# The first pass of each MLP takes two column blocks by seven products, sums of products kept apart, SBUF laid out with pads

## The chip, the cores and the metric

The kernel runs on one core of one Trainium2 chip. The engines that matter are TensorE (PE in the profile; PEld is its loading of weights), VectorE (DVE), ScalarE (ACT), GpSimd (POOL, almost unused) and SyncE (SP), whose queue issues nearly all transfers. The metric is device time in microseconds (us), less is better. The kernel before takes 2031.8 us, the median of three runs (2031.58 to 2032.2).

## The reference

Two layers over 256 tokens of width 2048, all in fp32. Each sub-layer ends in a layer norm over the scaled residual:

```python
for layer in range(DEPTH):                       # 2
    mix = short_conv_mixer(h, ...) if layer < N_A else mla_mixer(h, ...)
    h = layer_norm(ALPHA * h + mix, ln_g[layer, 0], ln_b[layer, 0])
    h = layer_norm(ALPHA * h + sq_relu_mlp(h, mlp_w1[layer], mlp_w2[layer]), ln_g[layer, 1], ln_b[layer, 1])

def sq_relu_mlp(x, w1, w2):                      # 2048 -> 8192 -> 2048
    return jnp.square(jax.nn.relu(x @ w1)) @ w2
```

The first layer mixes by a gated convolution, the second by latent attention with 16 heads. The change sits in the two MLPs (called idx 1 and idx 3 in the code, after the number of the norm that follows).

## The kernel before, in words

**Precision.** A matrix product is made from fp32r halves. `split` (L114) turns a tile into a high half (ScalarE, L116, a cast) and a low half (VectorE, L117, source minus high half); a product of two split operands is three matmuls: high with high, high with low, low with high (`dot`, L274 to L278). Where one operand has both halves side by side, the first two are one wide matmul (`mm_run`, L198).

**Weights.** All weights come once, as tiles of 128 x 1024 (512 KB), in the order of one list, `stream`. `take` (L166) hands out the next tiles and prepares those that follow, at most LOOK = 5 tiles ahead: `prepare` (L130) issues the load on SP's queue and splits the tile. There are five raw buffers and eight pairs of split ones.

**An MLP.** The 8192 hidden values are done in NQ = 8 passes (q) of QC = 8 chunks of 128. A pass first makes its eight chunks: each is 16 x 2 matmuls over the 2048 inputs (`products`, L265; L192 high, L196 low), taken out of PSUM, through relu and square, and split into `h` (`hidden`, L593). It then multiplies them into the output: `down` (L288) takes one block of 512 columns out of four, for both halves t of the tokens and all eight chunks: 16 products of three matmuls of 512 columns, 48 in all. `put` (L575) adds the result to `acc`, in the first pass by a copy on ScalarE (L577).

**The first pass (q = 0)** differs: the layer norm ahead of the MLP is not ready when its matmuls start, so the hidden products run on the un-normalised values with the norm's gain and offset as two additional columns (`mm_wide`, L219), and `ln.weighted` (L477 to L484) applies the norm's factors to the sums. These factors come from `ln.finish` (L448); the first hidden chunk is evacuated once they are there. Beside it the input itself is normalised for the later passes: `normal` (L567, which calls `ln.normal`, L465) for 16 chunks, each three VectorE steps (L470, L471, L475) and two on ScalarE (L472, L474). The code calls it once per hidden chunk after the first, and twice at each `put` of the pass.

**Seven products.** In the passes of FAST, before the change q = 1 to 6, blocks 0 and 1 are done together by a Strassen-like scheme: chunks are paired, a pair of chunks by two token halves is a 2 x 2 matrix, the weights of two chunks by two blocks another, and seven products replace eight. For one pair of chunks the weights' forms are made in `prepare` from two raw tiles: three splits of 1024 columns, a 1024-wide difference (L149), two 512-wide differences (L152, L155) and a split of 512. The hidden forms are four 128-wide sums (L605 to L608) and one split per pair. `down_fast` (L316) does 4 pairs x 7 products x 3 = 84 matmuls of 512 columns instead of 96, and `combine` (L642) adds the seven sums into the four places of `acc`.

**Ends of the MLPs.** The last pass is plain. In the first MLP `to_wide` (L658) turns the blocks back and starts the next norm (`prepare_all`, L680, subtracts a first mean from all 16 chunks of the residual; `begin` calls it at the head of the last pass). In the second MLP `to_out` (L911) normalises the output; its gain and offset, `gbt`, are loaded by GpSimd's queue (L914), and the residual is turned and added by `turn_residual` (L903) once per pass, ahead of the last block.

**Order.** The code is handed to a framework that schedules instructions for each engine from its own estimate of times and inserts semaphores; the order of each engine in the built program is then fixed, and an engine takes its instructions one after the other. PSUM has eight banks, handed out in turn (`psum`, L180).

## Time and profile before

| | |
|---|---|
| median of three runs | 2031.8 us |
| profiled execution | 2031.86 us, of which the span is 2030.0 us |
| TensorE busy | 2022.8 us |
| VectorE busy | 1637.1 us |
| ScalarE busy | 1186.2 us |
| first MLP's passes | 386 to about 1020 us |
| second MLP's passes | 1345 to 2030 us (the output's norm included) |
| granted TensorE clock | 1.00 in all stretches shown |

The profile is of one execution. Its busy times are per engine; its rows give the code's line (L117), the engine, the operation, and the program's names of the tiles written and read (`lo<-raw,hi`); "ps_u" are the sums of hidden products, "ps_d" those of `down`, "ps_f" those of the seven products, "raw" a weight tile as loaded, "hi" and "lo" its halves. A row of a view over time begins with the start in us and the duration; the bracket at the end says how long the engine was idle before and what ended it. A row of a view of one tile or line has count, shortest, median and longest duration in ns, and the first and last start. Matmuls overlap, so the step from one start to the next is shorter than the duration.

### The profile page before, as it was taken

The numbers are of one execution on the slowest core, as the hardware profiler recorded it, in microseconds if no ns is written. First come the engines' busy times: TensorE is split into PE (matmuls) and PEld (weight loads), VectorE is DVE, ScalarE is ACT, GpSimd is POOL, SyncE is SP. The second block draws the span as 40 slices with busy tenths as digits, with TensorE's granted clock in tenths as the row PEclk, the third lists the DMA queues.
The fourth block names the chain that finished last, engine by engine and source line by source line (L and its number), as shares of the span: only waits on it lengthen the run. The fifth ranks groups of instructions, "written<-read, shape, count | busy, mean of one in ns | idle before, by whom it ended". The sixth has DMA issues, their size and how long they took to land.

```text
span 2030.0 us, 30192 instructions
## 1 busy us (share of the span) xinstructions
PE 2022.8 (100%) x11240; PEld 1763.4 (87%) x11240; DVE 1637.1 (81%) x2559; ACT 1186.2 (58%) x1849; POOL 4.5 (0%) x25
## 2 busy tenths in 40 slices
PE   9999999999999999999999999999999999999998
PEld 8888888988888888888889998898888888888886
DVE  7667677778898988989788978776889898898966
ACT  6444445676566565655656655566656656565661
POOL 0000000000000000000000000000000000000000
PEclk9999999999999999999999999999999999999999
DMA  8666666564746557465654544656474664746573
GB/s 307 209 191 187 188 190 193 162 210 138 251 148 216 193 170 256 145 229 174 232 176 153 177 129 137 195 168 205 136 240 155 213 204 164 250 143 221 190 228 121
DMA packets 106851, 385.32 MB, mean 190 GB/s; under 512 B 11856, under 2 KB 12752, under 8 KB 106448
## 3 DMA queue, kind: packets, MB, share of 16 engines
q1 hardware_dynamic: 105984, 381.17, 57.9%
q0 software_dynamic: 576, 2.10, 0.3%
q8 instruction: 88, 1.44, 0.3%
q14 instruction: 59, 0.48, 0.1%
q10 hardware_dynamic: 144, 0.13, 0.0%
HBM read 381.25 MB, written 2.10 MB: 189 GB/s over the span
## 4 chain that ended last, share of the span: by engine, by line
PE 99%; DMA 0%; DVE 0%; issue 0%; SPq 0%; ACT 0%; DVEq 0%
PE ps_u L192 20%; PE ps_l L192 13%; PE ps_u L196 11%; PE ps_d L276 7%; PE ps_d L277 7%; PE ps_d L278 7%; PE ps_l L196 7%; PE ps_f L278 4%; PE ps_f L276 4%; PE ps_f L277 4%; PE ps_w L226 1%; PE ps_w L224 1%; PE ps_w L225 1%; PE ps_g L226 1%; PE ps_g L224 1%; PE ps_g L225 1%
## 5 line engine op out<-in xcount | busy, mean ns | idle before, releaser
L117 DVE TENSOR_TENSOR lo<-raw,hi 128x1024 fp32r<-128x1024 f32 x710 | 858.7, 1222 | 271.5 <-ACT hi L116 199.9
L116 ACT CAST hi<-raw 128x1024 fp32r<-128x1024 f32 x710 | 740.9, 1050 | 428.4 <-DMA raw<-in_w_dram 134.6
L192 PE MATMUL ps_u<-xhl,hi 128*128 128x512 f32 x1792 | 621.3, 391 | 0.0
L196 PE MATMUL ps_u<-xhl,lo 128*128 128x256 f32 x1792 | 500.1, 280 | 0.0
L192 PEld LDWEIGHTS ps_u<-xhl,hi 128*128 128x128 f32 x1792 | 334.4, 187 | 71.9
L196 PEld LDWEIGHTS ps_u<-xhl,lo 128*128 128x128 f32 x1792 | 339.2, 189 | 1.7
L276 PE MATMUL ps_d<-hi,h 128*128 128x512 f32 x640 | 249.9, 390 | 0.0
L277 PE MATMUL ps_d<-lo,h 128*128 128x512 f32 x640 | 249.3, 390 | 0.0
L278 PE MATMUL ps_d<-hi,h 128*128 128x512 f32 x640 | 249.2, 389 | 0.0
L192 PE MATMUL ps_l<-xhl_a,hi 128*128 128x512 f32 x704 | 244.1, 393 | 0.0
L196 PE MATMUL ps_l<-xhl_a,lo 128*128 128x256 f32 x704 | 195.5, 280 | 0.0
L192 PEld LDWEIGHTS ps_l<-xhl_a,hi 128*128 128x128 f32 x704 | 132.2, 188 | 29.8
L278 PEld LDWEIGHTS ps_d<-hi,h 128*128 128x128 f32 x640 | 120.2, 188 | 25.2
L276 PEld LDWEIGHTS ps_d<-hi,h 128*128 128x128 f32 x640 | 120.2, 188 | 25.0
L277 PEld LDWEIGHTS ps_d<-lo,h 128*128 128x128 f32 x640 | 120.2, 188 | 24.6
L196 PEld LDWEIGHTS ps_l<-xhl_a,lo 128*128 128x128 f32 x704 | 131.9, 188 | 0.2
L597 ACT ACTIVATE fh<-fh 128x256 f32<-128x256 f32 x112 | 46.5, 415 | 89.2 <-DVE fh L333 89.1
L116 ACT CAST hi_t<-raw_t 128x1024 fp32r<-128x1024 f32 x48 | 50.6, 1054 | 55.5 <-DVE raw_t L149 30.5
L192 PE MATMUL ps_l<-z,hi 128*128 128x512 f32 x240 | 82.4, 391 | 0.0
L226 PE MATMUL ps_w<-xd,hi 128*128 128x258 f32 x256 | 72.7, 285 | 0.0
L224 PE MATMUL ps_w<-xd,hi 128*128 128x258 f32 x256 | 72.6, 284 | 0.0
L225 PE MATMUL ps_w<-xd,lo 128*128 128x258 f32 x256 | 72.4, 283 | 0.0
(253 smaller groups left out, 3185.1 us busy)
## 6 DMA issues: line engine op xcount, KB each, us to landing
raw<-in_w_dram SPq DMA_DIRECT2D x416, 512.0 KB, 4.3
raw<-in_w2f_dram SPq DMA_DIRECT2D x96, 512.0 KB, 3.5
raw<-in_w_in_dram SPq DMA_DIRECT2D x88, 512.0 KB, 3.8
raw<-in_w_out_dram SPq DMA_DIRECT2D x32, 512.0 KB, 3.6
raw<-in_w_o_dram SPq DMA_DIRECT2D x32, 512.0 KB, 4.0
raw<-in_w_kv_dram SPq DMA_DIRECT2D x10, 512.0 KB, 3.6
raw<-in_w_q_dram SPq DMA_DIRECT2D x8, 512.0 KB, 4.4
raw<-in_w_uk_dram SPq DMA_DIRECT2D x8, 512.0 KB, 4.6
```

Source lines behind the costliest of these rows:

```text
L116: nc.scalar.copy(hi, src)
L117: nc.vector.tensor_tensor(lo, src, hi.bitcast(F32), ALU.subtract)
L192: nc.tensor.matmul(ps, w[blk // 8][0][:, blk % 8, :], x, start=first, stop=False)
L196: nc.tensor.matmul(ps[:, :T], w[blk // 8][1][:, blk % 8, :], x[:, :T], start=False, stop=last)
L224: nc.tensor.matmul(ps[:, :W], hi, x[k][:, :W], start=k == 0, stop=False)
L225: nc.tensor.matmul(ps[:, :W], lo, x[k][:, :W], start=False, stop=False)
L226: nc.tensor.matmul(ps[:, :W], hi, x[k][:, W:], start=False, stop=k == NC - 1)
L276: nc.tensor.matmul(ps, x[0], w[0], start=first, stop=False)
L277: nc.tensor.matmul(ps, x[0], w[1], start=False, stop=False)
L278: nc.tensor.matmul(ps, x[1], w[0], start=False, stop=last)
L597: nc.scalar.activation(f, f, AF.Relu)
```

## The change

- FAST becomes 0 to 6: the first pass too takes blocks 0 and 1 by seven products. Its order is block 2, then blocks 0 and 1, then block 3, and `mlp_stream` puts the weights in that order. The hidden forms of this pass are first kept unsplit in the tile `sums` and split after the hidden products, because their buffer is shared with the norm's wide input.
- The seven products are no longer combined in each pass. Four of them (1, 5, 7, 6) have sums of their own over the passes (`sums`), three (2, 3, 4) go straight into their places of `acc`: `keep`, seven additions per pass (copies on ScalarE in the first). `fold` combines them by six additions in the last pass.
- The hidden values of a pair of chunks lie in one tile and are split together (`pair_tile`, `hidden`).
- `normal` is called twice per hidden chunk of the first pass, and no longer at a `put`.
- `begin` is called for chunk 0 of the residual at the end of the first pass's hidden products, and for the others during those of the last pass.
- PSUM banks are named at each place; the order of the seven products is changed.
- SBUF: the big buffers are laid out at the start, with small pads between; the tables for the rotary positions and the mask are loaded at the start of the attention; `gbt` is loaded by SP's queue; `turn_residual` is called in passes 1 to 4, between blocks 2 and 3; a buffer of `rope` takes another tag; the scratch for dynamic transfers is set to 4096.

```diff
-FAST = range(1, NQ - 1)
+FAST = range(0, NQ - 1)
...
-    pmm = ctx.enter_context(tc.tile_pool(name="pmm", bufs=4, space=PS))
+    pmm = ctx.enter_context(tc.tile_pool(name="pmm", bufs=1, space=PS))
+
+
+    xres = act.tile([P, NC, T], F32, tag="xres", name="xres")
+    for tag, columns in (("c", 4096), ("pad0", 64), ("b", 8256), ("a1", 4128), ("pad1", 96), ("a2", 4128), ("pad2", 96)):
+        act.tile([P, columns], F32, tag=tag, name=f"at_{tag}")
+    small.tile([P, 32], F32, tag="pad", name="at_pad", bufs=1)
...
-            lead = 0
-            if q in FAST:
-                out += [(w2f[l, q, j, 0], w2f[l, q, j, 1]) for j in range(QC // 2)]
-                lead = 2
-            out += halves(w2[l, q, lead:])
+            plain = halves(w2[l, q, 2:] if q in FAST else w2[l, q])
+            fast = [(w2f[l, q, j, 0], w2f[l, q, j, 1]) for j in range(QC // 2)] if q in FAST else []
+            at = 0 if q or q not in FAST else len(plain) // 2
+            out += plain[:at] + fast + plain[at:]
...
-    def psum(name):
-        return Banks.next().tile([P, 512], F32, tag="mm", name=name)
+    def psum(name, bank=None):
+
+        bank = Banks.next() if bank is None else bank
+        return (pmm if bank < 4 else Banks.more).tile([P, 512], F32, tag=f"mm{bank}", name=name)
...
-    FACTORS = (("4", "22", "T4"), ("2", "12", "21"), ("3", "S4", "22"), ("1", "11", "11"),
-               ("6", "S2", "T2"), ("7", "S3", "T3"), ("5", "S1", "T1"))
-
-    def down_fast(x, forms):
...
+    OWN, KEPT = ("1", "5", "7", "6"), (2, 3, 4, 5, 6, 7, 0)
+
+
+    FACTORS = (("3", "S4", "22"), ("1", "11", "11"), ("5", "S1", "T1"), ("7", "S3", "T3"),
+               ("2", "12", "21"), ("6", "S2", "T2"), ("4", "22", "T4"))
+
+    def fast_products(ps, x, forms, j, n):
+
+        b, = take(1)
+        a = {"11": held(x[2 * j], 0), "12": held(x[2 * j + 1], 0), "22": held(x[2 * j + 1], 1)}
+        for i in range(4):
+            a[f"S{i + 1}"] = [forms[:, j, o, i * P:(i + 1) * P] for o in range(2)]
+        for p, l, r in FACTORS:
+            dot(ps[p], b[r], a[l], j == 0, j == n - 1)
...
                 nc.scalar.copy(block(n, t), ps)
-                for _ in range(2):
-                    normal()
             else:
                 nc.vector.tensor_tensor(block(n, t), block(n, t), ps, ALU.add)
+
+        sums = fast.tile([P, 4, BW], F32, name=f"sums{idx}")
+
+        def keep(p, ps):
+
+            at = sums[:, OWN.index(p)] if p in OWN else block(*{"2": (0, 0), "3": (1, 0), "4": (0, 1)}[p])
+            if q == 0 or q == FAST[0] and p in OWN:
+                nc.scalar.copy(at, ps)
+            else:
+                nc.vector.tensor_tensor(at, at, ps, ALU.add)
+
+        def first_pair(h, forms, banks):
+
+            n = QC // 2
+            ps = {p: psum(f"ps_f{p}", bank) for (p, _, _), bank in zip(FACTORS, banks)}
+            for j in range(n):
+                fast_products(ps, h, forms, j, n)
+            for p in ps:
+                keep(p, ps[p])
+
+        def fold():
+
+            s1, s5, s7, s6 = (sums[:, i] for i in range(4))
+            both = acc[:, 1, :2 * BW].rearrange("p (b c) -> p b c", b=2)
+            right = acc[:, :, BW:2 * BW]
+            two = lambda v: v.unsqueeze(1).to_broadcast([P, 2, BW])
+            for d, a, b in ((block(0, 0), block(0, 0), s1), (s6, s6, s1), (block(1, 0), block(1, 0), s6),
+                            (s7, s7, s6), (both, both, two(s7)), (right, right, two(s5))):
+                nc.vector.tensor_tensor(d, a, b, ALU.add)
+                yield
...
+            def pair_tile(m):
+
+                if m % 2 == 0:
+                    pool = (act, "ab") if q and m % 4 else (fast, "fq" if m % 4 else "fp")
+                    t = pool[0].tile([P, 2 * T], F32, tag=pool[1], name="fp")
+                    pair.append(t.rearrange("p (i t) -> p i t", i=2))
+                return pair[-1]
...
-                put_split(h[m], f)
...
+                if both is None:
+                    put_split(h[m], f)
+                elif m % 2:
+                    at = ht[:, m - 1:m + 1, :]
+                    split(at[:, :, :T], at[:, :, T:], both)
+                    j = m // 2
+                    sf = fast.tile([P, 4 * P], F32, tag="sf", name="sf") if q else sums[:, j]
+                    form(j, sf)
+                    if q:
+                        split(forms[:, j, 0, :], forms[:, j, 1, :], sf)
...
                     if m > 0:
                         normal()
+                        normal()
+                normal()
+                normal()
+                if begin:
+                    begin(range(1))
                 acc = act.tile([P, 2, D], F32, tag="a1", name=f"acc{idx}")
+                forms = act.tile([P, QC // 2, 2, 4 * P], F32R, tag="a2", name=f"forms{idx}_{q}")
+                nc.gpsimd.memset(block(1, 1), 0.0)
+                for j in range(QC // 2):
+                    split(forms[:, j, 0, :], forms[:, j, 1, :], sums[:, j])
             else:
-                for m, ps in enumerate(products(QC, xhl, turned=None if q == NQ - 1 and begin else TURNED)):
+                folds = fold()
+                for m, ps in enumerate(products(QC, xhl, TURNED, (0, 1))):
                     hidden(m, ps, whole)
+                    if q == NQ - 1:
+                        next(folds, None)
+                        if begin:
+                            begin(range(max(2 * m, 1), 2 * m + 2))
...
-            if q in FAST:
-                combine(put, down_fast(h, forms))
-            for n in range(2 if q in FAST else 0, NB):
-                if n == NB - 1 and extra:
-                    extra(block, q - 1)
-                down(h, put, n)
...
+            if q == 0:
+                down(h, put, 2, (1, 7))
+                first_pair(h, forms, (2, 3, 4, 5, 6, 0, 7))
+                down(h, put, 3, (1, 2))
+            else:
+                first_pair(h, forms, KEPT)
+                for n, banks in ((2, (1, 2)), (3, (3, 4))):
+                    down(h, put, n, banks)
+                    if extra and n == 2 and q <= NB:
+                        for t in range(2):
+                            extra(block, q - 1, t, 5 + t)
...
-    def prepare_all():
-        for k in range(NC):
+    def prepare_chunks(chunks):
+        for k in chunks:
             ln.prepare(k)
...
+        cos_t = ap.tile([P, T], F32, name="cos_t")
+        sin_t = ap.tile([P, T], F32, name="sin_t")
+        mask_t = ap.tile([P, 3 * P], F32, name="mask_t")
+        for t, source in ((cos_t, cosT), (sin_t, sinT), (mask_t, mask)):
+            nc.sync.dma_start(t, source)
...
-            nc.gpsimd.dma_start(gbt[:, n, :], gb[n].partition_broadcast(P))
+            nc.sync.dma_start(gbt[:, n, :], gb[n].partition_broadcast(P))
```

More of the change, by code (lines that the diff above doesn't have):

```diff
@@ L108, in next @@
             cls.count += 1
-            return cls.more if cls.more is not None and cls.count % 8 >= 4 else pmm
+            return (cls.count - 1) % (4 if cls.more is None else 8)
     state = {"split": 0, "next": 0}
@@ L286, in wide_rows, with down @@
         return [v[:, 4 * kk:4 * kk + 4, :].rearrange("p a c -> p (a c)") for v in w]
-    def down(x, put, n):
-        ps = [psum("ps_d") for _ in range(2)]
+    def down(x, put, n, banks=(None, None), amid=None):
+        ps = [psum("ps_d", bank) for bank in banks]
         for j in range(len(x) // 2):
@@ L586, in mlp, with form @@
             forms = None
-            if q in FAST:
+            if q and q in FAST:
                 forms = act.tile([P, QC // 2, 2, 4 * P], F32R, tag="a2", name=f"forms{idx}_{q}")
-            if q == NQ - 1 and begin:
-                begin()
             pair = []
+            def pair_tile(m):
[4 more added lines that the diff above has]
+                return pair[-1]
+            def form(j, sf):
+                (a11, a21), (a12, a22) = ((pair[j][:, i, :P], pair[j][:, i, P:]) for i in range(2))
+                s1, s2, s3, s4 = (sf[:, i * P:(i + 1) * P] for i in range(4))
+                nc.vector.tensor_tensor(s1, a21, a22, ALU.add)
+                nc.vector.tensor_tensor(s3, a21, a11, ALU.subtract)
+                nc.vector.tensor_tensor(s2, s1, a11, ALU.subtract)
+                nc.vector.tensor_tensor(s4, a12, s2, ALU.subtract)
             def hidden(m, ps, evac, *func):
-                f = tmp.tile([P, T], F32, tag="fh", name="fh", bufs=3)
+                both = pair_tile(m) if q in FAST else None
+                f = both[:, m % 2, :] if both is not None else tmp.tile([P, T], F32, tag="fh", name="fh", bufs=3)
                 evac(ps, f, *func)
```

74 lines of the change are left out of this document (15 added, 59 removed).

## The prediction

> **What bounds the kernel now.** I read the busy times and the chain of waits first, to see which engine sets the end; then the busy time by stage, because the change sits in one stage of each MLP; then matmul starts and VectorE starts, which give the true step from one instruction to the next.
>
> ```profile
> span 2030.0 us, 30192 instructions
> PE 2022.8 (100%) x11240; PEld 1763.4 (87%) x11240; DVE 1637.1 (81%) x2559; ACT 1186.2 (58%) x1849; POOL 4.5 (0%) x25
> ...
> PE 99%; DMA 0%; DVE 0%; issue 0%; SPq 0%; ACT 0%; DVEq 0%
> ```
>
> TensorE is the chain from end to end; a matmul less is time less, and any wait put before a matmul is time more. The next view has the first pass of the first MLP (386 to 454.9), a later pass, and the same two of the second MLP.
>
> ```profile
> core 0: us, PE busy (x) PEld busy (x) DVE busy (x) ACT busy (x) POOL busy (x), PEclk, DMA share, GB/s
> 386.00:454.90 68.90, 68.90 (x403) 61.20 (x403) 55.05 (x101) 53.80 (x96) 0.00 (x0) 1.00 0.62 199
> 454.90:540.70 85.80, 85.80 (x438) 72.99 (x437) 72.33 (x101) 52.65 (x78) 0.00 (x0) 1.00 0.57 182
> ...
> 1345.00:1413.40 68.40, 68.40 (x401) 60.86 (x400) 54.87 (x97) 53.70 (x96) 0.00 (x0) 1.00 0.61 197
> 1413.40:1500.10 86.70, 86.70 (x446) 73.82 (x445) 74.50 (x104) 52.85 (x78) 0.00 (x0) 1.00 0.56 177
> ```
>
> TensorE never waits in any of the four. VectorE (DVE) is second: it is idle for about 14 us of the first pass and for 12 to 13 us of a later one. So the change must be judged by two sums for the first pass: its matmuls, and the VectorE work that must be done before its last matmuls.
>
> **TensorE's part.** The first pass gives up the ordinary form of two column blocks, 2 x 48 = 96 matmuls of 512 columns, for 4 pairs x 7 products x 3 = 84. A row gives the first and last start of a group.
>
> ```profile
> L276 PE MATMUL ps_d<-hi,h x64: 389/389/397, 410.9 to 453.8; 128*128 128x512 f32 x64
> L192 PE MATMUL ps_u<-xhl,hi x45: 389/391/400, 454.5 to 469.7; 128*128 128x512 f32 x45
> ...
> L276 PE MATMUL ps_d<-hi,h x64: 389/389/398, 1369.4 to 1412.3; 128*128 128x512 f32 x64
> L192 PE MATMUL ps_u<-xhl,hi x35: 389/391/400, 1413.0 to 1424.8; 128*128 128x512 f32 x35
> ...
> L276 PE MATMUL ps_f<-t,h x4: 394/395/395, 498.9 to 513.6; 128*128 128x512 f32 x4
> L276 PE MATMUL ps_d<-hi,h x32: 389/389/397, 518.5 to 539.6; 128*128 128x512 f32 x32
> ```
>
> The 192 ordinary matmuls take 454.5 - 410.9 = 43.6 us, 0.227 us each, in both MLPs (1413.0 - 1369.4). The 84 products of a later pass take 518.5 - 498.9 = 19.6 us, 0.233 us each. New second half: 96 x 0.227 + 19.6 = 41.4 us, a gain of 2.2 us per MLP, 4.4 us in all, if TensorE is fed. In the twelve later passes the order of factors and the buffers change, the number of matmuls does not: 0 us there.
>
> **VectorE's part in the first pass.** Steps between starts, not durations, are what an instruction costs a busy engine:
>
> ```profile
> 493.20 0.42 DVE L338 TENSOR_TENSOR h<-fh,h 128x256 fp32r<-128x256 f32 x1
> 493.54 0.29 DVE L605 TENSOR_TENSOR sf<-fh 128x128 f32<-128x128 f32 x1
> 493.74 1.22 DVE L149 TENSOR_TENSOR raw_t<-raw,raw 128x1024 f32<-128x1024 f32 x1
> 494.87 0.29 DVE L607 TENSOR_TENSOR sf<-sf,fh 128x128 f32<-128x128 f32 x1
> 495.07 0.42 DVE L333 TENSOR_TENSOR fh<-ps_u,t 128x256 f32<-128x256 f32 x1
> 495.41 0.29 DVE L608 TENSOR_TENSOR sf<-fh,sf 128x128 f32<-128x128 f32 x1
> 495.61 1.22 DVE L117 TENSOR_TENSOR lo<-raw,hi 128x1024 fp32r<-128x1024 f32 x1
> 496.74 0.69 DVE L117 TENSOR_TENSOR forms<-sf,forms 128x512 fp32r<-128x512 f32 x1
> 497.34 0.69 DVE L152 TENSOR_TENSOR raw<-raw,raw_t 128x512 f32<-128x512 f32 x1
> 497.95 0.29 DVE L606 TENSOR_TENSOR sf<-fh 128x128 f32<-128x128 f32 x1
> ```
>
> A 1024-wide step is 1.13 us, a 512-wide one 0.60, a 256-wide one 0.335, a 128-wide one 0.20. One pair of seven-product weights needs three 1024-wide splits, one 1024-wide difference, two 512-wide differences and a 512-wide split: 4 x 1.13 + 3 x 0.60 = 6.3 us, against 21 x 0.233 = 4.9 us of TensorE. A later pass survives that since its 44 us of hidden products ask VectorE for little and it runs ahead. The first pass is fuller: its products come with sixteen normalisations. Where VectorE's work of the pass begins:
>
> ```profile
> 388.35 0.76 DVE L482 TENSOR_TENSOR t<-ps_g,ab 128x256 f32<-128x256 f32 x2 [0.95 <-ACT ab L456]
> 389.02 0.87 DVE L483 SCALAR_TENSOR_TENSOR t<-ab,wgb,t 128x256 f32<-128x256 f32 x2
> 389.81 0.42 DVE L470 TENSOR_TENSOR nu<-xres,ab 128x256 f32<-128x256 f32 x1
> ...
> 1346.25 0.76 DVE L482 TENSOR_TENSOR t<-ps_g,ab 128x256 f32<-128x256 f32 x2 [0.20 <-ACT ab L456]
> ```
>
> It cannot begin before the norm's factors are there, at 388.35 and 1346.25, and nothing ahead of that is changed. (The two L483 steps take 389.81 - 389.02, 0.395 us each.) The built order of the changed program gives VectorE, from there to the first weight split of the last column block (the fourth block, 48 matmuls):
>
> - 1024-wide: 18 splits (6 plain, 12 of the four pairs) and 4 differences, 22 x 1.13 = 24.9
> - 512-wide: 4 splits of the hidden pairs, 4 of the forms, 12 of the weight pairs' small steps, 20 x 0.60 = 12.0
> - 256-wide: 16 normalisations x 3 and 8 evacuations, 56 x 0.335 = 18.8, and 8 x 0.395 = 3.2 for the evacuations' second step
> - 128-wide: 16 sums for the forms x 0.20 = 3.2
>
> That is 62.1 us. In the first MLP ten 256-wide steps of the next norm stand among them (the start of the residual, done at once in the last pass before), 3.4 us more: 65.5.
>
> TensorE reaches the same point, fed, after 410.9 - 388.35 = 22.5 us of hidden products, 10.9 us of the third block and 19.6 us of the seven products: 53.0 us (53.5 with the mean that now stands here in the first MLP). So VectorE is 12 us late in the first MLP and 9 us in the second (there too 1369.4 - 1346.25 + 10.9 + 19.6 = 53.7). By the same count the kernel before asks 14 x 1.13 + 8 x (2 x 0.335 + 0.395) + 16 x 1.0 = 40.4 us in 454.5 - 10.9 - 388.35 = 55.3: that is its idle time, and it is overspent. The lead of five weight tiles that the queue allows doesn't help: it is VectorE's own work of this pass that is late, counted from its first instruction.
>
> Hand-offs come on top. ScalarE makes the high halves:
>
> ```profile
> 403.62 1.03 ACT L116 CAST hi<-raw 128x1024 fp32r<-128x1024 f32 x1
> 404.56 0.40 ACT L337 CAST h<-fh 128x256 fp32r<-128x256 f32 x1
> 404.86 0.60 ACT L472 ACTIVATE xres<-nu,vec 128x256 f32<-128x256 f32 x1
> 405.37 0.59 ACT L474 ACTIVATE xhl<-nu,vec 128x256 fp32r<-128x256 f32 x1
> ```
>
> Its steps are 0.94 (cast), 0.30 and 0.51 us, and in the stretch it has 17 casts, 32 normalising steps, 16 short steps for the hidden values and 16 half-width ones: 16.0 + 16.3 + 5.6 + 8.2 = 46 us, under VectorE's 62. What is left is each pair's chain: the second difference waits for the end of the first (1.22 where the step is 1.13), the third for the end of the second. I take 0.25 us a pair in the second MLP (1.0) and 0.3 us in all in the first, whose ten fillers stand in those gaps. Ends for this term: 0, and one cast of 1.03 us uncovered in each of four pairs (4.1 per MLP). I stay near the lower end, as VectorE had queued work in the rows above and did not pause.
>
> First MLP: 388.35 + 65.5 + 0.3 = 454.1; behind it 46 matmuls of the last block (two need only the high half and are ahead), 10.4 us: next pass at 464.5 against 454.5, +10.0. Second: 1346.25 + 62.1 + 1.0 = 1409.3, 47 matmuls, 10.7: 1420.0 against 1413.0, +7.0. The 2.2 us per MLP that TensorE saves are inside these differences. Nothing gives the time back later, since TensorE has no waits later.
>
> **Costed at nothing, with the cover.** Per later pass ten additions and a copy become seven additions: VectorE gets freer where it already does not bind. Six fold additions (four 512-wide, two 1024-wide, 4.7 us) enter the last pass, whose hidden products take 44 us and ask VectorE for about 30; uncovered they would cost 4.7 per MLP. The pair-wise split of the hidden values delays one half by a product (5.5 us), and the values are first used a block later. The transposes and the turned residual move within the pass, unchanged in number. The transfers: the seven-product weights come by the same bytes, and a load lands in 3.5 us, while a slot is freed a pair (6.3 us) ahead.
>
> ```profile
> raw<-in_w2f_dram SPq DMA_DIRECT2D x96, 512.0 KB, 3.5
> ...
> L914 POOL DMA_DIRECT2D gbt<-in_gb_dram x4: 527/529/662, 1976.1 to 1977.8; - x4
> ...
> L931 DVE TENSOR_TENSOR acc<-acc,gbt x3: 687/690/691, 1989.8 to 2017.5; 128x512 f32<-128x512 f32 x3
> ...
> gbt<-in_gb_dram POOLq DMA_DIRECT2D x4, 512.0 KB, 9.5
> ```
>
> The output's gain and offset move from POOL's queue to SP's: four loads that wait, as now, until TensorE has left the last hidden input (1976.1), with four weight loads of the last blocks behind them on SP. The cover is 13.7 us to their first use (1989.8) against 9.5 for a landing, and five weight tiles of lead for the four behind (5 x 12 x 0.227 = 13.6 us): 0; if that goes, one landing, 3.5 to 9.5 us.
>
> The three rotary and mask loads move on SP into the first MLP's last pass; in the built order the first waits for a product of the pass before, done by then: 0. The buffers' new addresses and pads: no row prices them. The nearest is the step of a product, 0.233, against 0.227 of a plain matmul: were all 1008 products of the later passes to run at 0.227, 6 us would go; as much the other way is the other end. I take 0.
>
> **Sum.** +10.0 + 7.0 = +17.0 on the profiled execution's 2031.86 us (span 2030.0 and 1.9 around it; the median of the runs is 2031.8): 2049.
>
> [...] The rows above speak against a full serial step here: L607 starts at 494.87 while L149 (493.74, 1.22 long) ends at 494.96. With whole durations instead of steps, 0.09 us more for each of 132 and 122 instructions, the two sums would be 77.4 and 73.1 and the time 2049 + 11.9 + 11.0 = 2072. I give that 0.03.
>
> **Rivals.**
>
> Not slower: VectorE's lead covers the pass. It decides if VectorE has its work before the last block done in 53 us where I count 62 to 65, that is if ten or more of those steps (the normalisations are 16 us, and are only needed by the next pass) fall behind it in effect. For it: in twelve later passes the same pairs never made TensorE wait. Against it: the engine takes its instructions in the built order, and the normalisations stand ahead. Time: 2031.9 - 4.4 = 2027.5. Chance 0.09; 0.04 that a part of it just cancels, within 0.2% of before (4 us, about what a measurement of this kernel can tell from no change).
>
> Starved as forecast, and the addresses give the products 0.227 us: 2043. Chance 0.07.
>
> Starved with the hand-offs at their upper end, 4.1 per MLP in place of 0.3 and 1.0: +6.9, 2056. For it: ScalarE is itself at 46 of 62 us, and the order has it wait for TensorE in between. Chance 0.12.
>
> The clock falls while TensorE starves.
>
> ```profile
> 2020.00:2030.00 10.00, 4.77 (x11) 1.63 (x9) 5.65 (x14) 0.20 (x1) 0.00 (x0) 1.00 0.28 105
> ```
>
> Against it stands this row: 10 us with TensorE busy for less than half of it, and the granted clock is 1.00. Were the 84 products to run at half rate in the starved stretch, they would need 39 us where VectorE leaves them 31: +8 per MLP, 2065. Chance 0.03. [...]
>
> **How the numbers follow.** The forecast has 0.62. Slower: 0.62 + 0.07 + 0.12 + 0.03 + 0.03 = 0.87; the same 0.04; faster 0.09. The range takes in the cases from 2043 to 2056 with the unknown addresses around them: 2040 to 2060, 0.81.
>
> **What would show it.** The next pass's first hidden product starts near 464.5, and 17 us more after the second MLP's; VectorE is busy without a break from 388 to 454; TensorE's idle time rises by some 20 us, in the two first passes, waiting for L122 (the split's low half) of the seven-product weights. Later passes stay at 85.8 and 86.7 us. Wrong: the first passes without waits, or waits in the later passes, in the last pass (folds) or at the end (the output's factors).

## The result, and the profile after

The changed kernel takes 2045.5 us (median of four runs, 2044.9 to 2045.9) against 2031.7 for the kernel before: 1.0067 times as long, 95% interval 1.0054 to 1.0079. The forecast was 2049, +17; it is +13.8. The profiled execution took 2045.85 us. The profile's page of the changed kernel:

```profile
span 2044.1 us, 30089 instructions
PE 2020.8 (99%) x11216; PEld 1757.7 (86%) x11216; DVE 1652.6 (81%) x2547; ACT 1192.3 (58%) x1811; POOL 3.3 (0%) x23
...
PE 94%; DVE 4%; DMA 1%; ACT 1%; issue 0%; SPq 0%; DVEq 0%; ACTq 0%
```

The span is 14.1 us longer although TensorE is busy for 2.0 us less: it now waits, and VectorE has come into the chain that sets the end. Its waits by what ended them (total us, times, longest):

```profile
PE ps_f L283 <- ACT hi_t L121: 6.4, 5, 1.6
PE ps_f L284 <- DVE lo L122: 2.7, 1, 2.7
PE ps_d L283 <- ACT h L121: 2.4, 1, 2.4
PE mu0p L394 <- DVE xres L392: 1.5, 1, 1.5
PE ps_g L199 <- ACT hi L121: 1.4, 1, 1.4
PE ps_f L283 <- ACT hi L121: 1.3, 6, 0.2
PE offset L1007 <- DVE udiag L1005: 1.2, 1, 1.2
PE ps_d L283 <- ACT mu L395: 1.1, 1, 1.1
```

All but two of these (the opening's `ps_g` and the end's `offset`) lie in the two first passes. Where the time went is read from starts. Of the kernel before and then of the changed one: the first matmul of each MLP's hidden products (`ps_g`) and the first of the pass behind (`ps_u`, whose rows of before stand in the prediction):

```profile
L224 PE MATMUL ps_g<-xd,hi x48: 276/282/292, 363.2 to 380.3; 128*128 128x258 f32 x48
L224 PE MATMUL ps_g<-xd,hi x48: 276/282/292, 1321.9 to 1338.9; 128*128 128x258 f32 x48
```

```profile
L231 PE MATMUL ps_g<-xd,hi x48: 276/282/292, 364.6 to 381.7; 128*128 128x258 f32 x48
L199 PE MATMUL ps_u<-xhl,hi x128: 389/391/400, 467.4 to 511.5; 128*128 128x512 f32 x128
L231 PE MATMUL ps_g<-xd,hi x48: 276/282/292, 1330.9 to 1348.0; 128*128 128x258 f32 x48
L199 PE MATMUL ps_u<-xhl,hi x128: 389/391/400, 1430.5 to 1474.5; 128*128 128x512 f32 x128
```

| stretch | before | after | difference | forecast |
|---|---|---|---|---|
| up to the first MLP | 363.2 | 364.6 | +1.4 | 0 |
| its first pass | 91.3 | 102.8 | +11.5 | +10.0 |
| its later passes, attention, w_o | 867.4 | 863.5 | -3.9 | 0 |
| first pass of the second MLP | 91.1 | 99.6 | +8.5 | +7.0 |
| its later passes and the end | 617.0 | 613.6 | -3.4 | 0 |

The first passes lose 20.0 us, 3 more than forecast; everything else gains 5.9 that were not forecast. In the first passes TensorE stands while VectorE does not:

```profile
389.80:412.40 22.60, 22.60 (x191) 22.60 (x190) 22.45 (x59) 22.32 (x47) 0.53 (x1) 1.00 0.25 85
412.40:457.00 44.60, 35.94 (x139) 25.64 (x138) 43.59 (x76) 29.36 (x47) 0.00 (x0) 0.96 0.37 107
467.40:552.60 85.20, 85.20 (x437) 72.90 (x436) 75.42 (x99) 55.60 (x77) 0.00 (x0) 1.00 0.67 229
...
1378.50:1419.60 41.10, 34.10 (x135) 24.98 (x133) 40.45 (x64) 28.16 (x45) 0.00 (x0) 0.96 0.36 116
```

The columns are those of the first windows in the prediction. Behind the hidden products of the first MLP (412.4 to 457.0) VectorE is busy for 43.6 of 44.6 us, TensorE for 35.9. VectorE's own rows carry the sum: the first step with the norm's factors, one pair's chain, and the first splits of the last column block, in the first MLP and then in the second.

```profile
389.77 0.76 DVE L480 TENSOR_TENSOR t<-ps_g,ab 128x256 f32<-128x256 f32 x2 [0.95 <-ACT ab L454]
...
433.81 1.23 DVE L122 TENSOR_TENSOR lo<-raw,hi 128x1024 fp32r<-128x1024 f32 x1 [1.01 <-ACT hi L121]
434.95 0.69 DVE L122 TENSOR_TENSOR t<-raw,t 128x512 fp32r<-128x512 f32 x1
435.56 1.22 DVE L154 TENSOR_TENSOR raw_t<-raw,raw 128x1024 f32<-128x1024 f32 x1
436.69 0.42 DVE L399 SCALAR_TENSOR_TENSOR xres<-xres,mu 128x256 f32<-128x256 f32 x1
437.03 0.69 DVE L157 TENSOR_TENSOR raw<-raw,raw_t 128x512 f32<-128x512 f32 x1
...
455.48 2.35 DVE L122 TENSOR_TENSOR lo<-raw,hi 128x1024 fp32r<-128x1024 f32 x2
...
1355.32 0.76 DVE L480 TENSOR_TENSOR t<-ps_g,ab 128x256 f32<-128x256 f32 x2 [0.23 <-ACT ab L454]
...
1412.45 1.22 DVE L154 TENSOR_TENSOR raw_t<-raw,raw 128x1024 f32<-128x1024 f32 x1
1413.70 0.69 DVE L157 TENSOR_TENSOR raw<-raw,raw_t 128x512 f32<-128x512 f32 x1
1414.43 0.69 DVE L160 TENSOR_TENSOR raw<-raw 128x512 f32<-128x512 f32 x1
1415.49 1.23 DVE L122 TENSOR_TENSOR lo_t<-raw_t,hi_t 128x1024 fp32r<-128x1024 f32 x1 [0.37 <-ACT hi_t L121]
...
1418.37 2.35 DVE L122 TENSOR_TENSOR lo<-raw,hi 128x1024 fp32r<-128x1024 f32 x2
```

With the 1.13 us of that first split: 455.48 + 1.13 - 389.77 = 66.8 us, forecast 65.8; 1418.37 + 1.13 - 1355.32 = 64.2, forecast 63.1. The later passes are shorter because a product of the seven takes less. These rows are of the second pass of the first MLP, the seven products and the blocks behind them; from the first start to the first start the 84 products take 530.9 - 511.8 = 19.1 us, 0.227 each, where they took 19.6:

```profile
L283 PE MATMUL ps_f<-hi,forms x8: 389/389/391, 511.8 to 529.5; 128*128 128x512 f32 x8
L283 PE MATMUL ps_d<-hi,h x32: 389/389/389, 530.9 to 552.0; 128*128 128x512 f32 x32
```

### The profile page after: what moved, and what is told of

Same layout as the page of the kernel before. It is cut to its first block, busy times and chain, and to the rows that moved or that the text cites. A ratio compares the mean times of both kernels' runs of the same rounds, so it can differ in the third digit from the quotient of the medians.

```text
span 2044.1 us, 30089 instructions
## 1 busy us (share of the span) xinstructions
PE 2020.8 (99%) x11216; PEld 1757.7 (86%) x11216; DVE 1652.6 (81%) x2547; ACT 1192.3 (58%) x1811; POOL 3.3 (0%) x23
## 4 chain that ended last, share of the span: by engine, by line
PE 94%; DVE 4%; DMA 1%; ACT 1%; issue 0%; SPq 0%; DVEq 0%; ACTq 0%
PE ps_u L199 20%; PE ps_l L199 13%; PE ps_u L203 11%; PE ps_l L203 7%; PE ps_d L283 6%; PE ps_d L284 6%; PE ps_d L285 6%; PE ps_f L284 4%; PE ps_f L285 4%; PE ps_f L283 4%; PE ps_g L233 1%; PE ps_g L231 1%; PE ps_g L232 1%; PE ps_w L231 1%; PE ps_w L233 1%; PE ps_w L232 1%
## 5 line engine op out<-in xcount | busy, mean ns | idle before, releaser
L283 PE MATMUL ps_d<-hi,h 128*128 128x512 f32 x576 | 225.5, 392 | 3.5 <-ACT h L121 2.4
L284 PE MATMUL ps_d<-lo,h 128*128 128x512 f32 x576 | 224.9, 390 | 0.0
L285 PE MATMUL ps_d<-hi,h 128*128 128x512 f32 x576 | 224.7, 390 | 0.1
L283 PEld LDWEIGHTS ps_d<-hi,h 128*128 128x128 f32 x576 | 108.4, 188 | 26.9 <-ACT h L121 2.8
L285 PEld LDWEIGHTS ps_d<-hi,h 128*128 128x128 f32 x576 | 108.6, 188 | 23.2 <-DVE h L122 0.5
L284 PEld LDWEIGHTS ps_d<-lo,h 128*128 128x128 f32 x576 | 108.6, 188 | 22.2
L121 ACT CAST hi_t<-raw_t 128x1024 fp32r<-128x1024 f32 x56 | 58.8, 1051 | 57.1 <-DVE raw_t L154 50.4
L199 PE MATMUL ps_l<-z,hi 128*128 128x512 f32 x240 | 83.9, 398 | 0.0
L638 ACT ACTIVATE fp<-fp 128x256 f32<-128x256 f32 x96 | 40.0, 416 | 71.6 <-DVE fp L340 71.2
L154 DVE TENSOR_TENSOR raw_t<-raw,raw 128x1024 f32<-128x1024 f32 x56 | 68.3, 1220 | 7.4 <-DMA raw<-in_w2f_dram 7.3
```

Of the source, the lines that this page charges most:

```text
L121: nc.scalar.copy(hi, src)
L154: nc.vector.tensor_tensor(t.rearrange(two, a=2), b12.unsqueeze(1).to_broadcast([P, 2, BW]), r1.rearrange(two, a=2), ALU.subtract)
L199: nc.tensor.matmul(ps, w[blk // 8][0][:, blk % 8, :], x, start=first, stop=False)
L283: nc.tensor.matmul(ps, x[0], w[0], start=first, stop=False)
L284: nc.tensor.matmul(ps, x[0], w[1], start=False, stop=False)
L285: nc.tensor.matmul(ps, x[1], w[0], start=False, stop=last)
```

## The experiments

Theory A is that of the forecast: the first passes starve because VectorE has more to do there, ahead of the last block, than TensorE gives it time for. Against it stood B (something else in the change costs the time) and C (not the amount but the chain within a weight pair binds). Theories P and O are on the products' step.

**One part undone.** The first passes in the ordinary way, all else as changed.

```diff
-FAST = range(0, NQ - 1)
+FAST = range(1, NQ - 1)
...
-                down(h, put, 2, (1, 7))
-                first_pair(h, forms, (2, 3, 4, 5, 6, 0, 7))
-                down(h, put, 3, (1, 2))
+                for n, banks in enumerate(((1, 7), (2, 3), (4, 5), (6, 7))):
+                    down(h, put, n, banks)
```

> The changed kernel with one part undone: the first pass of each MLP takes its four column blocks in the ordinary way again (FAST from 1); kept sums, pads, banks, order of products, early normalisations and the early mean stay. Theory A (the first passes starve because VectorE has 62 to 66 us of work there, everything else is small): the first passes go back to the length of before, 91.3 and 91.1 us from the start of the norm's products to the next pass, plus at most 2 us for the early mean in the first MLP; what is left of the change is +1.4 (convolution's output) and 12 x -0.54 (later passes), so 2026 to 2028 us, below the kernel before. Rival B (the kept sums, the pads or the early normalisations cost something themselves): 2032 or more.

Measured 2026.55 us, ratio to the kernel before 0.9974 (0.9964 to 0.9984). The same stretch as above, in this run:

```profile
388.10:455.70 67.60, 67.58 (x390) 59.59 (x389) 58.25 (x113) 52.86 (x96) 0.00 (x0) 1.00 0.62 195
```

TensorE never waits, from the first step with the norm's factors to the next pass. The seven products of the first pass cost 18.9 us, and the rest of the change gains 5.2. B is out. No version below that leaves nothing out is faster, and it is faster than both kernels.

**The same work, later.** Seven normalisations are asked for beside the hidden products, the other nine behind the last block.

```diff
                     if m > 0:
                         normal()
-                        normal()
-                normal()
-                normal()
...
                 down(h, put, 3, (1, 2))
+                for _ in range(NC):
+                    normal()
```

> The changed kernel, but only seven of the sixteen normalisations of the first pass are asked for beside the hidden products; the other nine are asked for behind the last column block, and in the built order most of them stand behind that block's weight splits. No work is taken away. Theory A: VectorE's work ahead of the last block's first split falls from 64.2 to 54.8 us in the first MLP and from 60.9 to 54.2 in the second, so the next passes begin about 9.5 and 6.7 us earlier: 2029 to 2031 us. If the nine then hold up the next pass's first product, up to 3 us of it per MLP is given back: up to 2036. Rival C (the starved stretch is bound by the chain from one difference of a weight pair to its cast and to the next, not by how much VectorE has to do ahead): 2042 to 2046, since nothing in the pairs' chain is changed.

Measured 2029.56 (ratio 0.9990, 0.9981 to 1.0000). The next passes start at:

```profile
L199 PE MATMUL ps_u<-xhl,hi x34: 389/392/504, 458.1 to 469.7; 128*128 128x512 f32 x34
L199 PE MATMUL ps_u<-xhl,hi x75: 389/392/497, 1413.1 to 1439.8; 128*128 128x512 f32 x75
```

That is 9.3 and 17.4 us earlier; 16 us come back and no step was taken away. C is out as the limit: the pairs' chain was not touched. A small part is given back as expected, as the first product of the next pass waits for normalised input (L473, 0.7 us).

**The work left out.** VectorE's steps of the normalisations are taken away, ScalarE's stay; the later passes thus get no normalised input, and only the time is of use.

```diff
-                ln.normal(k, xhl[k])
+                ln.normal_less(k, xhl[k])
...
+        def normal_less(self, m, dst):
+            g, b = self.gain(m)
+            d = xres[:, m, :]
+            nc.scalar.activation(dst[:, :T], d, AF.Identity, bias=b, scale=g)
+            nc.scalar.activation(d, d, AF.Identity, bias=b, scale=g)
+            nc.gpsimd.memset(dst[:, T:].bitcast(F32), 0.0)
```

> The changed kernel with VectorE's share of the sixteen normalisations of each first pass left out (the two steps of the norm's factors and the low half, 16 x 3 steps of 256); ScalarE's two steps per chunk stay and GpSimd clears the low halves, so the normalised input of the later passes is left out of the computation. Theory A: VectorE's work ahead of the last block is 47.6 and 44.3 us, under TensorE's 53: no waits in the first passes but for the early mean, 2020 to 2023 us. Rival C (chain within the pairs): waits on the differences' casts stay, 2035 or more.

Measured 2020.8 in one run. The first passes have no wait left, and take 453.4 - 363.8 = 89.6 and 1405.4 - 1316.9 = 88.5 us, 1.7 and 2.6 less than before: TensorE's 2.2 us per MLP are real when it is fed.

**The mean in the last pass.**

```diff
-                if begin:
-                    begin(range(1))
...
-                            begin(range(max(2 * m, 1), 2 * m + 2))
+                            begin(range(2 * m, 2 * m + 2))
```

> The changed kernel, but the mean of the residual's first chunk and the subtractions behind it are asked for in the last pass of the first MLP instead of the first. Theory A: VectorE's work ahead of the last block in the first MLP falls by ten steps of 256 (3.4 us, 64.2 to 61.2 by the built order), and the two waits around the mean's matmul (1.5 and 1.1 us) go; the second MLP is unchanged: 2042 to 2043 us. Rival: those ten steps stand in gaps that the pairs' chain leaves anyway, and the two waits are only moved to the pairs: 2045 to 2046.

Measured 2044.72: 0.8 less, nearer to the rival. The two waits around the mean are gone, and a wait of 3.3 us on a low half stands in their place:

```profile
PE ps_f L283 <- ACT hi_t L121: 6.4, 6, 1.6
PE ps_f L284 <- DVE lo L122: 6.0, 2, 3.3
```

But the small gain does not show that the rival holds, because the clock differs too. Rows of the first MLP in this run: VectorE's first splits of the last block, TensorE's first matmul of that block, and two stretches with the granted clock.

```profile
452.13 2.35 DVE L122 TENSOR_TENSOR lo<-raw,hi 128x1024 fp32r<-128x1024 f32 x2
...
454.90 0.39 PE L283 MATMUL ps_d<-hi,h 128*128 128x512 f32 x1
...
426.00:436.00 10.00, 8.74 (x25) 6.25 (x26) 9.90 (x13) 5.16 (x6) 0.00 (x0) 0.66 0.33 107
450.00:455.00 5.00, 4.79 (x15) 3.81 (x15) 4.49 (x5) 4.84 (x8) 0.00 (x0) 0.66 0.60 185
```

VectorE's first step with the norm's factors is at 389.11 here, so the stretch to the end of the first split is 452.13 + 1.13 - 389.11 = 64.2 us, 2.7 less than the 66.8 of the changed kernel: of the ten steps' 3.4 us, 0.7 had stood in gaps, as the forecast had it. TensorE begins the last block at 454.90, 1.6 us behind the end of that split. It was still at the products of the last pair, with a granted clock of 0.66 over the 5 us there. From 430 to 434 us the granted clock of this run was 0.50; counted at that, 0.66 over 5 us is 3.4 us at half rate, which by an estimate cost TensorE 1.7. Counted so, the clock is at half for 17 us of the two first passes (6.8 and 3.4 in the first MLP, where 44.6 us from 412.4 have 0.89, and 6.8 in the second, where 41.1 us from 1378.5 have 0.92), against 6.8 in the changed kernel. So the ten steps are worth up to 2.7 us, an estimate from these rows; no run shows what the move gives at full clock.

**Both moves.** The deferred normalisations and the late mean, by the edits shown:

```diff
-                            begin(range(max(2 * m, 1), 2 * m + 2))
+                            begin(range(2 * m, 2 * m + 2))
...
                 down(h, put, 3, (1, 2))
+                for _ in range(NC):
+                    normal()
```

> The variant with nine deferred normalisations, and the mean of the residual in the last pass as well: the best form of the seven-product first pass that moves work without giving it to another engine. By the built order VectorE has 54.2 us ahead of the last block's first split in both MLPs. Theory A: as the deferred variant (2029.6) or up to 1 us less, 2028.5 to 2029.6, still above the variant with an ordinary first pass (2026.6), because the pass as a whole asks VectorE for about 66 us and TensorE for 64. Rival: once the mean is gone the first pass runs fed and the 12 matmuls come through, 2024 or less.

Measured 2029.83 (ratio 0.9989, 0.9979 to 0.9998): the late mean adds nothing, and 2026.6 is not reached. The best form of the change's first pass that was tried stays 3 us behind an ordinary one. In the profiled executions the first passes take 93.1 and 91.4 us (in the first the granted clock was 0.92 over 20.6 us, which counted as above is some 3.3 us at half rate), with an ordinary first pass 92.0 and 91.4; most of the difference lies in the stretches behind them (864.9 and 615.6 us against 863.6 and 613.6), where the deferred normalisations are now done. The 12 matmuls less per MLP bring nothing here.

**Weight differences on GpSimd.**

```diff
-        nc.vector.tensor_tensor(t.rearrange(two, a=2), b12.unsqueeze(1).to_broadcast([P, 2, BW]),
+        eng = nc.gpsimd if state.get("first") else nc.vector
+        eng.tensor_tensor(t.rearrange(two, a=2), b12.unsqueeze(1).to_broadcast([P, 2, BW]),
...
-        nc.vector.tensor_tensor(b12, b22, t[:, :BW], ALU.subtract)
+        eng.tensor_tensor(b12, b22, t[:, :BW], ALU.subtract)
...
-        nc.vector.tensor_tensor(t4, b21, b12, ALU.subtract)
+        eng.tensor_tensor(t4, b21, b12, ALU.subtract)
...
+            state["first"] = q == 0
```

> The changed kernel with the differences of the first pass's weight pairs (one of 1024 columns and two of 512 per pair) made on GpSimd instead of VectorE: nothing is left out, 9.4 us of VectorE's work per first pass changes its engine. Theory A: VectorE's work ahead of the last block falls to 54.5 and 51.5 us; if GpSimd takes no longer than twice VectorE's time, the pairs' chain keeps up and the two first passes lose 8 to 9 us each of their waits: 2027 to 2031 us. Rival C (the chain from difference to cast to difference within a pair is what binds): 2044 or more, the more the slower GpSimd is. No row here shows how long GpSimd takes.

Measured 2059.95, 14.5 us more. GpSimd's group of the 1024-wide differences (busy us, mean ns), and then rows of GpSimd and of VectorE from the same moments:

```profile
L155 POOL TENSOR_TENSOR raw_t<-raw,raw 128x1024 f32<-128x1024 f32 x8 | 24.2, 3020 | 2.9 <-DVE lo_t L122 2.2 <-DMA raw<-in_w2f_dram 0.6 <-issue 0.2
```

```profile
430.31 2.07 POOL L161 TENSOR_TENSOR raw<-raw 128x512 f32<-128x512 f32 x1 [15.33 <-ACT hi L121]
432.34 3.37 POOL L155 TENSOR_TENSOR raw_t<-raw,raw 128x1024 f32<-128x1024 f32 x1
```

```profile
430.01 1.22 DVE L122 TENSOR_TENSOR lo_t<-raw_t,hi_t 128x1024 fp32r<-128x1024 f32 x1
431.14 2.31 DVE L122 TENSOR_TENSOR lo<-raw,hi 128x1024 fp32r<-128x1024 f32 x1
433.38 2.88 DVE L122 TENSOR_TENSOR t<-raw,t 128x512 fp32r<-128x512 f32 x1
```

The same difference takes 3.0 us instead of 1.22, and the two splits of VectorE shown here that begin while GpSimd is at work take 2.31 instead of 1.22 and 2.88 instead of 0.69. The first of them begins at 431.14 and ends at 433.45, 1.07 us behind the end of GpSimd's step (432.38); the second ends at 436.26, 0.55 behind the end of GpSimd's next (435.71). That is as if each began only when GpSimd had ended; these rows show the times, not the cause. Thus this run doesn't decide between A and C: VectorE was not relieved.

**All three moves.** Deferred normalisations, late mean, differences on GpSimd, by the edits shown:

```diff
+        eng = nc.gpsimd if state.get("first") else nc.vector
...
+                            begin(range(2 * m, 2 * m + 2))
...
                 down(h, put, 3, (1, 2))
+                for _ in range(NC):
+                    normal()
```

> The changed kernel with three moves and no work left out: nine of the sixteen normalisations asked for behind the last block, the first pass's weight differences on GpSimd, the mean of the residual in the last pass. Theory A: VectorE has 45.3 us ahead of the last block in both MLPs, under TensorE's 53, so the first passes run fed and their 12 matmuls less per MLP come through: 2031.7 + 1.4 - 6.5 - 4.4 = 2022 us, under the variant with an ordinary first pass (2026.6). Rival C, or a slow GpSimd: 2030 or more.

Measured 2054.32, a miss, by the author's estimate at least in part for the same reason: in the run before, a 128-wide step of VectorE that began beside GpSimd (L631, at 410.20) took 2.50 us, where it took 0.28 with GpSimd idle (at 422.07). TensorE's longest waits in this run are two of 3.4 us for ScalarE's copies of finished products (L585); how far GpSimd is behind those was not followed up.

**Where the products' step comes from.** Five runs move the pads or the order of the products; of the layout the fences show only the entries that change.

```diff
-(("c", 4096), ("pad0", 64), ("b", 8256), ("a1", 4128), ("pad1", 96), ("a2", 4128), ("pad2", 96))
+(("c", 4096), ("b", 8256), ("a1", 4128), ("a2", 4128))
-    small.tile([P, 32], F32, tag="pad", name="at_pad", bufs=1)
```

> The changed kernel with the pads between the big buffers taken out; buffers, banks and order of the seven products stay. It asks where the 0.54 us per later pass comes from (the step of a product went from 0.233 to 0.227) and the 1.4 us that the convolution's output lost (its 512-wide matmul went from 391 to 398 ns). Theory P (addresses): the later products go back to 0.233, 12 x 84 x 0.006 = 6.1 us more, and the convolution's output may go back to 391 ns, 1.4 us less: 2050 to 2052 us. Theory O (order of the seven products and their banks): steps stay at 0.227, 2044 to 2046.

Measured 2051.73 (2049.0 to 2055.4). Both steps go back. Three fences: the group of the convolution's output matmuls in the changed kernel (busy us, mean ns), the same without pads, and a later pass's products without pads.

```profile
L199 PE MATMUL ps_l<-z,hi 128*128 128x512 f32 x240 | 83.9, 398 | 0.0
```

```profile
L198 PE MATMUL ps_l<-z,hi 128*128 128x512 f32 x240 | 82.4, 391 | 0.0
```

```profile
L282 PE MATMUL ps_f<-hi,forms x8: 390/392/404, 510.4 to 528.5; 128*128 128x512 f32 x8
L282 PE MATMUL ps_d<-hi,h x32: 389/389/395, 529.9 to 551.0; 128*128 128x512 f32 x32
```

(529.9 - 510.4) / 84 = 0.232. The order of the products is not it:

```diff
-    FACTORS = (("3", "S4", "22"), ("1", "11", "11"), ("5", "S1", "T1"), ("7", "S3", "T3"),
-               ("2", "12", "21"), ("6", "S2", "T2"), ("4", "22", "T4"))
+    FACTORS = (("4", "22", "T4"), ("2", "12", "21"), ("3", "S4", "22"), ("1", "11", "11"),
+               ("6", "S2", "T2"), ("7", "S3", "T3"), ("5", "S1", "T1"))
```

> The changed kernel with the seven products of a pair in the order of the kernel before (4, 2, 3, 1, 6, 7, 5), pads and layout as changed. Theory P (addresses): the step stays at 0.227 and the later passes are as in the changed kernel; the first passes may shift by 1 or 2 us, because the product that needs a pair's last difference then comes first: 2045 to 2049 us. Theory O (order): the step of the later products goes back to 0.233: 6.1 us more, 2051 or more.

Measured 2047.44; ten of the twelve later passes keep 0.226 or 0.227, the first and the last have 0.232 and 0.231, which stays unexplained. The three others start from the variant with an ordinary first pass:

```diff
-("pad0", 64), ("b", 8256), ("a1", 4128), ("pad1", 96)
+("b", 8256), ("a1", 4128), ("pad1", 160)
```

> The variant with an ordinary first pass, and the first pad (64 columns ahead of the convolution's output) moved behind the next buffer but one, so that all that lies behind it keeps its address. It asks which pad did what. Theory P1 (the 398 ns of the convolution's output hang on that buffer's own address, the 0.227 us of the later products on what lies further back): 391 ns again and 0.227 kept, 1.4 us less than the variant: 2025 us. Rival P2 (the products' step hangs on the same address): step 0.232 and 391 ns, 12 x 84 x 0.005 = 5 us more and 1.4 less: 2030. Rival P3 (neither moves): 2026.5.

Measured 2026.59, both steps as in the variant (398 ns, 0.227): 64 columns more or less ahead of the buffers before the forms' don't matter.

```diff
-("pad1", 96), ("a2", 4128), ("pad2", 96)
+("a2", 4128), ("pad2", 192)
```

> The variant with an ordinary first pass, the first pad left where it is and the other one between the big buffers moved behind the last, so that only the buffer of the hidden forms (and of the norm's second half) lies 96 columns lower. Theory P1: the later products' step depends on the address of what they read or of what lies near it, the forms among it: 0.232, 5 us more than the variant, 2031.5, with the convolution's output at 398 ns. Rival P2 (the products' step hangs on the address of the big buffer behind the first pad): 0.227 and 2026.5.

Measured 2030.84, both steps as without pads: the convolution's output matmuls take 391 ns again (82.4 us), and a later pass has

```profile
L283 PE MATMUL ps_f<-hi,forms x8: 390/398/404, 499.9 to 517.9; 128*128 128x512 f32 x8
L283 PE MATMUL ps_d<-hi,h x32: 389/389/389, 519.3 to 540.4; 128*128 128x512 f32 x32
```

So it is the 96 columns ahead of `a2`, where the hidden forms lie: (519.3 - 499.9) / 84 = 0.231. Of that pad a third does as well:

```diff
-("pad1", 96), ("a2", 4128), ("pad2", 96)
+("pad1", 32), ("a2", 4128), ("pad2", 160)
```

> The variant with an ordinary first pass, the pad ahead of the hidden forms' buffer cut from 96 to 32 columns and the last pad grown by as much. Theory: the two steps (398 ns of the convolution's output, 0.227 us of the products) depend on that buffer's address. If they depend on it in the same way they go together, as with 0 and 96 columns: either 398 and 0.227 (2026.6) or 391 and 0.232 (2030.8). If not, one place may have both good, 391 and 0.227: 2025.1.

Measured 2026.84, with 398 ns and 0.227: the two steps go together, one good and the other bad. Why the convolution's output, whose operand `z` lies in another buffer, answers to this place stays open; beside those matmuls half of the norm's wide input is written to `a2` (`ln.widen("a1", "a2")`), but no run tests that.

## Why the prediction was right

**Direction, place and mechanism** were as forecast: VectorE's work ahead of the last block, counted from the norm's factors, against 53 us of TensorE. The run without VectorE's normalising steps, the run with them later and the ordinary first pass move the time by -25, -16 and -19 us.

**The two sums.** The count of VectorE's steps was right; the term that was mis-sized is the hand-offs, "What is left is each pair's chain ... I take 0.25 us a pair in the second MLP (1.0) and 0.3 us in all in the first": the stretches are 1.0 and 1.1 us longer than that. The chain itself costs what was taken: in the second MLP 1.25 us from a pair's first difference to the second and 0.73 to the third (1412.45, 1413.70, 1414.43), where free steps are 1.13 and 0.60, so 0.25 a pair. What was put at nothing are VectorE's waits for ScalarE's casts. In the first MLP one of them, the idle 1.01 us ahead of 433.81, is about all of the excess. In the second two (0.37 us ahead of 1415.49 and 0.27 ahead of 1376.19) stretch their steps by 0.8 in sum, most of it. Both stay well under the upper end of 4.1. (ScalarE's sum of 46 us takes 0.35 for a short step, where the row shows 0.30; 0.8 us less changes nothing.) Behind the first split TensorE takes 10.8 and 11.0 us to the next pass, where 10.4 and 10.7 were counted. In all about +1.5 per MLP. Whole durations in place of steps, the case of 2072, no run shows: VectorE's split at 433.81 lasts 1.23 us, and the next step starts 1.14 behind its start.

**The ten fillers.** The forecast counted the next norm's ten steps at their full 3.4 us and let them fill 0.7 us of gaps. The run with the late mean bears that out for VectorE, which is 2.7 us sooner without them; TensorE gained only 1.0 us of it in that pass, where the granted clock was lower as well (0.89 from 412.4 to 457.0, against 0.96).

**The name of the wait.** The forecast had TensorE wait for the pairs' low halves. It waits longest, 6.4 us in sum, for the cast of a pair's first difference (`hi_t`), because its order has the high halves first. Behind the cast stands VectorE's difference: the one at 1412.45 ends at 1413.67, and TensorE's matmul on its cast starts at 1415.51. In that last pair of the pass ScalarE adds to it, for it copies finished products first and begins the cast only at 1414.40.

**Addresses, "I take 0".** This was the larger miss, though the lower end given, 6 us, was what came: 12 x 0.5 = 6 of the 7.3 us that the later stretches gained. The rival with its 0.07 for 2043 is thus half of what happened. The 1.4 us lost ahead of the first MLP were in no rival: the convolution's output matmuls alone take 83.9 - 82.4 = 1.5 us more, and the opening's wait on a cast is 1.4 us where it was 0.6; what gave part of that back was not followed up. (In the ten other profiled executions with the same 398 ns the stretch ends between 363.7 and 364.6.) That 2049 came so close is in part luck, because two misses of opposite sign meet: the starvation was put 3.0 us too small, and the 5.9 us that the rest gained were missing.

**The clock** fell after all, twice and briefly. Two stretches of the changed kernel. The granted clock was 0.50 from 426.0 to 429.0 and from 1395.5 to 1398.0, so 0.66 over 5 us is 3.4 us at half rate:

```profile
416.50:425.00 8.50, 3.36 (x12) 1.57 (x11) 8.50 (x25) 7.94 (x16) 0.00 (x0) 1.00 0.21 62
425.00:430.00 5.00, 5.00 (x15) 3.92 (x16) 5.00 (x10) 1.31 (x2) 0.00 (x0) 0.66 0.02 3
...
1389.50:1396.00 6.50, 2.77 (x9) 1.36 (x8) 6.43 (x10) 3.85 (x7) 0.00 (x0) 0.93 0.00 0
```

Eight matmuls took 3.39 us from 425.67 and 3.58 from 1395.02, where at 0.227 each they take 1.82; the differences, 1.6 and 1.8 us, bound the loss of each. Little of it can have reached the end, since behind each of the two TensorE waits again for the casts of a later pair (1.17 and 1.62 us in the first MLP, 0.98 and 1.65 in the second). In the run with the late mean the clock fell right ahead of the last block (0.66 from 450 to 455 us), and there TensorE began the block 1.6 us behind VectorE's split. No gap of TensorE in the changed kernel's two first passes was longer than 2.7 us; what makes the clock fall is not shown.

**Costed at nothing and so it was:** later passes without waits, the folds, the turned residual, the output's factors on SP. No wait appears there.

## What to carry to other kernels

Before a product is traded for additions, sum the work of the engine that makes the additions over the stage where it is fullest, from the first instruction that can't start sooner to the point where the other engine needs it; a share of 81% over the span said nothing about a pass that had 62 us of work for 53. When such a stage is over-full, moving what is needed last behind what is needed first can win back most of the loss; here it won back 16 of 19 us and did not beat the form that asks for less. When a run that was to price one step gains less than its sum, look at the granted clock before the sum is given up. And when a buffer moves, compare the step of the same matmul in both traces before anything else is explained.

## What the runs showed of the hardware that was not expected

- The 512-column matmuls of the seven products had a step of 0.227 or of 0.231 to 0.233 us, by where in SBUF a buffer begins; 32 or 96 columns more ahead of `a2` gave the better one for the seven products and the worse one (398 for 391 ns of duration) for the convolution's output. No run separates the cause.
- With GpSimd at work, VectorE's 512-wide split took 2.88 us for 0.69. An idle engine was no help here, as the busy one's steps beside it took longer.
- In the changed kernel the clock fell to half (0.50 granted) for 3.4 us after stretches in which TensorE was busy for less than half of the time (3.4 of 8.5 us, 2.8 of 6.5), without any gap over 2.7 us. In the run with the late mean it was at half for 17 us in sum, counted from the granted clock.
